# Head norms of q and k: sums of squares on TensorE transposes, or on 32x32 turns in VectorE and a DRAM round trip

## The chip, the cores and the metric

The kernel runs on one core of one Trainium2 chip. A core has five engines with queues of their own: PE (TensorE, matrix products; PEld is its weight load), DVE (VectorE), ACT (ScalarE), POOL (GpSimd) and SP (SyncE, which here issues nearly all DMAs). Each works through its own list of instructions in order and waits on semaphores for the others. The metric is the device time of one execution in microseconds. The median of three runs of the kernel before is 1879.47 us (1879.23 to 1879.48).

## The reference

One layer of a decoder trunk on 512 tokens with 2048 channels. What matters here is the QK normalisation in two of its three token mixers:

```python
def _rms_norm(x, g):
    xf = x.astype(jnp.float32)
    y = xf * lax.rsqrt(jnp.mean(xf * xf, axis=-1, keepdims=True) + EPS)
    return (y * g.astype(jnp.float32)).astype(x.dtype)

h = _rms_norm(x, norm1_g[l])
proj = h @ w_in[l]
aq, ak, av, bu, bg, cq, ck, cv = jnp.split(proj, splits, axis=-1)
aq = _rms_norm(aq.reshape(B, S, A_HEADS, HEAD_DIM), a_q_g[l])     # 8 heads x 64
ak = _rms_norm(ak.reshape(B, S, A_HEADS, HEAD_DIM), a_k_g[l])
out_a = _dilated_mixture(aq, ak, av)
out_b = _conformer_conv(bu, bg, ...)
cq = _rms_norm(cq.reshape(B, S, C_Q_HEADS, HEAD_DIM), c_q_g[l])   # 16 heads x 64
ck = _rms_norm(ck.reshape(B, S, C_KV_HEADS, HEAD_DIM), c_k_g[l])  # 2 heads x 64
out_c, _ = _band_attention(cq, ck, cv, C_WINDOW - 1, sinks=c_sinks[l])
x = x + jnp.concatenate([out_a, out_b, out_c], axis=-1) @ w_out[l]
h2 = _rms_norm(x, norm2_g[l])
x = x + (jax.nn.silu(h2 @ w_gate[l]) * (h2 @ w_up[l])) @ w_down[l]
```

So each token needs, for each head of q and k, one over the root of the sum of 64 squares.

## The kernel before, in words

Activations are held with channels on the 128 partitions and the 512 tokens along the free axis, in tiles of 128x512. Every product is done in three float32r matmuls (`mm3`, lines 315 to 317): high by high, high by low, low by high part. The program runs through the first normalisation, the 30 projections of the list `PROJ`, the output projection (32 units), gate and up in a Strassen-like form (line 1081), and down (lines 1339 to 1341).

Each projection makes one tile of 128 output channels, which for q and k is two heads of 64. The 17 tiles that need head norms are `ck`, `cq0` to `cq7`, `ak0` to `ak3` and `aq0` to `aq3`. A projection is two units of weights with 8 steps each; after every second step the kernel calls `ticks.tick()`, so a projection has 8 ticks. Everything that isn't a projection is hung on these ticks: `ticks.after(n, f)` puts `f` into the program n + 1 ticks later. A tick fixes only where an instruction stands in the order of its engine, not when it runs; an engine that is late stays late, and PE stops only where it reads something that isn't there yet.

`head_scales` does this for each of the 17 tiles: ACT copies the bank to `raw` (line 578); SQ = 3 ticks later PE turns `raw` in four 128x128 transposes into a bank (`flip`, line 583), so that tokens lie on partitions; a tick later ACT squares it (line 588); a tick later DVE sums groups of 64 (line 593) and adds 64 times epsilon (line 595); a tick later POOL takes the power of -1/2 (line 600). The result `r` is 128 tokens x 4 token blocks x 2 heads.

For q (`do_q`), `r` is used as the scale of the scores: DVE first reads it in `top` (line 741), ACT in `exps` (line 751). The q tile itself is split in high and low parts, and two DMAs (lines 628, 629, `twin`) put the low part below the high one. For k (`do_k`) two ticks after the power ACT spreads `r` over 64 columns (`widen`, line 640), a tick later PE turns it back (line 647), DVE multiplies `raw` by it (line 652), ACT and DVE split it (657, 662), and eight DMAs (line 670) lay out the copies. `attention` takes its first tick from `box["q at"]`, `box["k at"]` and the head before it; the scores are on lines 731 and 732.

SP's queue carries the weight loads (`pump`, line 254), these `twin` DMAs, and near the end of the stage the loads of x for the residual (line 913). A weight load waits for DVE to have finished with the buffer (line 264). DVE also runs the 124 taps of the depthwise convolution (lines 524, 526) over the whole stage, about one every two ticks.

Of the kernel before, what the change touches and what calls it, by code (L numbers as in the profile page):

```python
# [9 lines left out]
F32 = mybir.dt.float32  # L10
# [3 lines left out]
AF = mybir.ActivationFunctionType  # L14
ALU = mybir.AluOpType

P = 128
T = 512
NT = T // P
D = 2048  # L20
KT = D // P
HD = 64
# [13 lines left out]
TAP_PAUSE = (197, 211)  # L36


SQ, VD, TD, EV = 3, 4, 2, 1


C_TICKS = (1, 6, 2, 2, 2, 2, 5, 1, 3)
# [74 lines left out]
def kernel(ctx: ExitStack, tc: tile.TileContext, xT, wi, wo, wgu, wd, cst_in, outT):  # L117
    nc = tc.nc
    cp = ctx.enter_context(tc.tile_pool(name="consts", bufs=1))
# [16 lines left out]
    ticks = Ticks()  # L136

    def slot(name, dt=F32, cols=T):
        return sp.tile([P, cols], dt, name=name, tag="s")

    def bank(name, cols=T, pool="banks"):
        return psum[pool].tile([P, cols], F32, name=name, tag="b")
# [51 lines left out]
    for p in GU_ORDER:  # L194
        for m in range(2):
# [4 lines left out]
    bufs = {"A": dict(zip(("21", "11", "s", "22"), ("21a", "22a", "sa", "22b"))),  # L200
            "B": dict(zip(("21", "11", "s", "22"), ("21b", "11", "12", "sb")))}
# [6 lines left out]
    for t, (g, r) in enumerate(DOWN):  # L208
# [7 lines left out]
        for k in ("21A", "11A", "21B", "11B", "22A", "22B", "12A", "12B"):  # L216
            c = k[2]
# [20 lines left out]
        bufs = {c: {"21": b["s"], "s": b["21"], "11": b["22"], "22": b["11"]} for c, b in bufs.items()}  # L238

    splits = {}  # L240
    at = {"entry": 0, "split": 0, "use": 0}
# [95 lines left out]
    b = bank("idle")  # L337
    for i in range(WARM):
        nc.tensor.matmul(b, idle, idle[:, None, :].to_broadcast([P, NT, P]), start=True, stop=True)
    b = idle = None  # L340

    nhalf = cp.tile([P, 8], F32, name="nhalf")
# [3 lines left out]
    ident = cp.tile([P, P], F32, name="ident")  # L346
# [18 lines left out]
        return b  # L365

    def small(name, cols=NT):
        return cp.tile([P, cols], F32, name=name, tag="small", bufs=24)


    mult_a = slot("mult_a")
# [47 lines left out]
    def token_scale(acc, n, name, b=None):  # L419

        v, r = small(name + "v"), small(name + "r")
        if b is None:

            t, b = bank(name), v
            for i in range(NT):
                nc.tensor.transpose(t[:, i * P:(i + 1) * P], acc[:, i * P:(i + 1) * P], ident)
            nc.vector.tensor_reduce(v, t.rearrange("p (a b) -> p a b", b=P), axis=mybir.AxisListType.X, op=ALU.add)
        else:
            stat_rows(b[:, :, None], acc, ones)
        nc.vector.tensor_scalar(v, b, 1.0 / n, EPS, op0=ALU.mult, op1=ALU.add)  # L430
        nc.gpsimd.tensor_tensor(r, v, nhalf[:, :NT], op=ALU.pow)  # L431
        return v, r
# [46 lines left out]
    c64 = cp.tile([P, NT], F32, name="c64")  # L479
# [7 lines left out]
    def project(name):  # L487
        b = bank(name, pool="tiles")
        for half in range(2):
            wh, wl = next_unit()  # L490
            for kk in range(8):
                k = 8 * half + kk
                s = slice(kk * P, (kk + 1) * P)
                mm3(b, wh[:, s], wl[:, s], h_hi[k], h_lo[k], k == 0, k == KT - 1)
                if kk == 3:
                    lows_now()
                if kk % 2 == 1:
                    ticks.tick()
        return b
# [75 lines left out]
    def head_scales(b, name, then):  # L575

        raw = slot(name + "raw")
        nc.scalar.copy(raw, b)

        def flip():  # L580
            b2 = bank(name + "f")
            for i in range(NT):
                nc.tensor.transpose(b2[:, i * P:(i + 1) * P], raw[:, i * P:(i + 1) * P], ident)
            ticks.after(1, square, b2)

        def square(b2):
            sq = slot(name + "sq")
            nc.scalar.activation(sq, b2, AF.Square)
            ticks.after(1, total, sq)

        def total(sq):
            v = cp.tile([P, NT, 2], F32, name=name + "v", tag="hsv", bufs=3)
            nc.vector.tensor_reduce(v.rearrange("p a b -> p (a b)"), sq.rearrange("p (a b) -> p a b", b=HD),
                                    axis=mybir.AxisListType.X, op=ALU.add)
            nc.vector.tensor_add(v, v, c64[:, :, None].to_broadcast([P, NT, 2]))
            ticks.after(1, power, v)

        def power(v):
            r = cp.tile([P, NT, 2], F32, name=name + "r", tag="hsr", bufs=4)
            nc.gpsimd.tensor_tensor(r, v, nhalf.rearrange("p (a b) -> p a b", b=2), op=ALU.pow)  # L600
            then(r)

        ticks.after(SQ, flip)
        return raw

    def do_q(box, b, name):
        def then(r):
            box["rq"] = r

        raw = head_scales(b, name, then)  # L610
        box["q at"] = ticks.now + SQ + 6

        q = [slot(f"{name}{h}", F32R) for h in range(2)]
        lo = slot(f"{name}l", F32R)
        box["q"] = q
        one, two = HALF

        def high():
            nc.scalar.copy(q[0], raw)
            nc.scalar.copy(q[1][one], raw[two])  # L620
            ticks.after(1, low)

        def low():
            nc.vector.tensor_sub(lo, raw, q[0].bitcast(F32))
            ticks.after(1, twin)

        def twin():
            nc.sync.dma_start(q[0][two].bitcast(F32), lo[one].bitcast(F32))
            nc.sync.dma_start(q[1][two].bitcast(F32), lo[two].bitcast(F32))
        ticks.after(1, high)  # L630

    def do_k(box, b, name, gi):
        def then(r):
            ticks.after(2, widen, r)

        raw = head_scales(b, name, then)
        box["k at"] = ticks.now + SQ + TD + 12
        def widen(r):
            wide = slot(name + "wide")
            nc.scalar.copy(wide.rearrange("p (a b c) -> p a b c", a=NT, b=2),  # L640
                           r[:, :, :, None].to_broadcast([P, NT, 2, HD]))
            ticks.after(1, flip, wide)

        def flip(wide):
            b2 = bank(name + "t")
            for i in range(NT):
                nc.tensor.transpose(b2[:, i * P:(i + 1) * P], wide[:, i * P:(i + 1) * P], ident)
            ticks.after(1, scale, b2)

        def scale(b2):  # L650
            k = slot(f"{name}k")
            nc.vector.scalar_tensor_tensor(k, raw, gqk[:, gi:gi + 1], b2, op0=ALU.mult, op1=ALU.mult)
            ticks.after(1, high, k)

        def high(k):
            hi = slot(f"{name}hi", F32R)
            nc.scalar.copy(hi, k)
            ticks.after(1, low, k, hi)

        def low(k, hi):  # L660
            lo = slot(f"{name}lo", F32R)
            nc.vector.tensor_sub(lo, k, hi.bitcast(F32))
            ticks.after(1, twin, hi, lo)

        def twin(*parts):
            box["k"] = [[slot(f"{name}{'hl'[i]}{h}", F32R) for i in range(2)] for h in range(2)]
            for h in range(2):
                for to, part in zip(box["k"][h], parts):
                    for at in HALF:
                        nc.sync.dma_start(to[at].bitcast(F32), part[HALF[h]].bitcast(F32))  # L670
# [209 lines left out]
    for name in PROJ[HEAD4:]:  # L880
        kind, what, j = name[0], name[1], name[2:]
        if name == PROJ[-2]:
            for n, row in enumerate(ROWS[:8]):
                ticks.after(6 + n, split_mix, row)
        b = project(name)
        if kind == "b":
            ticks.after(0, glu_u if what == "u" else glu, int(j), b)
            continue
        if kind == "c":
            box = Heads(shared) if j else shared  # L890
        else:
            box = boxes.setdefault(j, {})
        if what == "k":
            do_k(box, b, name, 1 if kind == "c" else 0)
        elif what == "v":
            do_v(box, b, name)
        else:
            do_q(box, b, name)
        if what == "q":
            if kind == "a":  # L900
                boxes.pop(j)
            attention(kind, box, mix, kind + j, (int(j), int(j) + 8) if kind == "c" else None)
    b = box = boxes = shared = None
# [81 lines left out]
    for half in range(2):  # L985
        for i, n in enumerate(OUT_ORDER[half]):
            if half == 1 and i == 2:
                open_banks(banks=2, high=2)
            b = bank(f"o{half}_{n}", pool="tiles")
            wh, wl = next_unit()  # L990
            for kk in range(8):
                k = 8 * half + kk
# [22 lines left out]
    b = m_hi = m_lo = r1b = mult_a = bias_a = bias_c = None  # L1015
# [33 lines left out]
    flip = [1]  # L1049
# [177 lines left out]
    for g in range(2 * NP):  # L1227
        p, m = GU_ORDER[g // 2], g % 2
# [257 lines left out]
```

## Time and profile before

| | us |
|---|---|
| median of the runs | 1879.47 |
| span of the profiled execution | 1877.5 |
| PE busy | 1871.1 |
| PEld busy | 1603.6 |
| DVE busy | 1469.3 |
| ACT busy | 1345.5 |
| POOL busy | 1066.3 |

The profiled execution lasted 1877.5 us from its first to its last instruction; the runs' median is 2.0 us above that. Start times below are in us from the start of the span. A row of a timeline gives the start, the length, the engine, the line, the operation with what it writes and reads, the count of merged instructions, and in brackets how long the engine stood idle before it and for whom. The granted TensorE clock is full in every slice of the page.

### The profile page before, as it was taken

Reading aid. Unit: us, or ns where it says so; the run is one execution under the profiler, and the core shown is the slowest. Engines: PE = TensorE matmul, PEld = TensorE weight load, DVE = VectorE, ACT = ScalarE, POOL = GpSimd, SP = SyncE. Lnnn points to the kernel's source line nnn. Section 1 sums busy time; section 2 is a strip of 40 time slices with the busy share of each in tenths; the row PEclk is TensorE's granted clock in tenths of the full one; section 3 lists DMA queues with packets and bytes.
Section 4 is the critical chain, followed back from the end, with each engine's and each line's share of the span. In section 5 each row is a group of like instructions: output and inputs, shape, how many; then the busy total and the mean of one; then the engine's idle time right before and its main releaser. Section 6 shows DMA issues by size and latency. Waiting matters only on the chain.

```text
span 1877.5 us, 28378 instructions
## 1 busy us (share of the span) xinstructions
PE 1871.1 (100%) x9722; PEld 1603.6 (85%) x9722; DVE 1469.3 (78%) x2468; ACT 1345.5 (72%) x1872; POOL 1066.3 (57%) x666
## 2 busy tenths in 40 slices
PE   9999999999999999999999999999999999999999
PEld 7888888888888888888888888888888888888887
DVE  6789978999679777777777777778777778677777
ACT  6356645453457888888878888788888877778775
POOL 0111011010002888788878888787787788879775
PEclk9999999999999999999999999999999999999999
DMA  7232242333342445555555554555546967666545
GB/s 271 92 126 81 82 122 89 113 117 125 119 145 98 146 145 173 157 177 185 158 167 157 181 184 158 164 157 186 167 152 234 328 219 240 224 212 238 199 142 113
DMA packets 201089, 307.11 MB, mean 164 GB/s; under 512 B 62960, under 2 KB 112752, under 8 KB 200944
## 3 DMA queue, kind: packets, MB, share of 16 engines
q1 hardware_dynamic: 200800, 305.28, 50.4%
q8 instruction: 77, 1.26, 0.3%
q14 instruction: 68, 0.56, 0.1%
q10 hardware_dynamic: 144, 0.01, 0.0%
HBM read 243.89 MB, written 52.95 MB: 158 GB/s over the span
## 4 chain that ended last, share of the span: by engine, by line
PE 99%; DMA 0%; SPq 0%; ACT 0%; DVE 0%; issue 0%; DVEq 0%
PE out L1081 46%; PE out L1339 7%; PE out L1341 7%; PE out L1340 7%; PE o L315 3%; PE o L316 3%; PE o L317 3%; PE cq L315 2%; PE cq L317 2%; PE cq L316 2%; PE av L315 1%; PE ak L315 1%; PE av L317 1%; PE aq L317 1%; PE aq L315 1%; PE ak L317 1%
## 5 line engine op out<-in xcount | busy, mean ns | idle before, releaser
L1081 PE MATMUL out<-h,wh 128*128 128x512 f32 x2464 | 588.6, 391 | 0.0
L1081 PEld LDWEIGHTS out<-h,wh 128*128 128x128 f32 x2464 | 453.1, 188 | 87.1
L1081 PEld LDWEIGHTS out<-h,wl 128*128 128x128 f32 x2464 | 315.9, 191 | 12.0
L1081 PE MATMUL out<-h,wl 128*128 128x256 f32 x2464 | 319.7, 283 | 0.0
L1339 PE MATMUL out<-wh,a 128*128 128x512 f32 x620 | 240.6, 388 | 0.0
L1341 PE MATMUL out<-wh,a 128*128 128x512 f32 x620 | 240.6, 388 | 0.0
L1340 PE MATMUL out<-wl,a 128*128 128x512 f32 x620 | 240.6, 388 | 0.0
L286 ACT CAST wh<-w 128x1024 fp32r<-128x1024 f32 (+2 forms) x94 | 96.7, 1030 | 119.6 <-PE o L316 51.2
L264 DVE TENSOR_TENSOR wl<-w,wh 128x1024 fp32r<-128x1024 f32 (+2 forms) x95 | 112.8, 1187 | 37.2 <-ACT wh L286 37.0
L1341 PEld LDWEIGHTS out<-wh,a 128*128 128x128 f32 x620 | 116.4, 188 | 23.9
L1340 PEld LDWEIGHTS out<-wl,a 128*128 128x128 f32 x620 | 116.4, 188 | 23.8
L1339 PEld LDWEIGHTS out<-wh,a 128*128 128x128 f32 x620 | 116.4, 188 | 23.7
L1349 DVE TENSOR_TENSOR y<-y,out 128x512 f32<-128x512 f32 x164 | 106.3, 683 | 25.3 <-PE out L1341 23.5
L526 DVE SCALAR_TENSOR_TENSOR y<-bu,cst,y 128x511 f32<-128x511 f32 (+14 forms) x120 | 87.6, 730 | 0.4
L315 PE MATMUL cq<-hh,wh 128*128 128x512 f32 x128 | 51.1, 400 | 0.0
L315 PE MATMUL o<-mh_c,wh 128*128 128x512 f32 x128 | 51.1, 400 | 0.0
L317 PE MATMUL cq<-hh,wl 128*128 128x512 f32 x128 | 50.1, 391 | 0.0
L317 PE MATMUL o<-mh_c,wl 128*128 128x512 f32 x128 | 50.0, 391 | 0.0
L316 PE MATMUL cq<-hl,wh 128*128 128x512 f32 x128 | 50.0, 391 | 0.0
L316 PE MATMUL o<-ml_c,wh 128*128 128x512 f32 x128 | 50.0, 390 | 0.0
L431 POOL TENSOR_TENSOR lvr<-lvv,nhalf 128x4 f32<-128x4 f32 x1 | 1.9, 1920 | 74.5 <-DVE lvv L430 74.5
L182 POOL TENSOR_TENSOR w('s', 'g0')_5681<-w('21', 'g0')_5527,w('22', 'g0')_5525 128x1024 f32<-128x1024 f32 x1 | 2.5, 2456 | 69.0 <-DVE wl L264 69.0
(3016 smaller groups left out, 4945.2 us busy)
## 6 DMA issues: line engine op xcount, KB each, us to landing
od<-a SPq DMA_DIRECT2D x154, 256.0 KB, 4.8
a<-od SPq DMA_DIRECT2D x154, 256.0 KB, 5.5
w<-in_wi SPq DMA_DIRECT2D x58, 512.0 KB, 3.5
w<-in_wo SPq DMA_DIRECT2D x32, 512.0 KB, 3.5
x<-in_xT SPq DMA_DIRECT2D x16, 256.0 KB, 6.9
xr<-in_xT SPq DMA_DIRECT2D x16, 256.0 KB, 3.7
x2d<-xr SPq DMA_DIRECT2D x16, 256.0 KB, 2.0
z<-x2d SPq DMA_DIRECT2D x64, 64.0 KB, 3.7
```

Source lines behind the costliest of these rows:

```text
L182: nc.gpsimd.tensor_add(out[:, :n], raws[key[a]][0][:, :n], raws[key[b]][0][:, :n])
L264: fn(*args)
L286: (nc.vector.tensor_copy if u == 0 else nc.scalar.copy)(hi[:, :n], t[:, :n])
L315: nc.tensor.matmul(out, wh, xh, start=start, stop=False)
L316: nc.tensor.matmul(out, wh, xl, start=False, stop=False)
L317: nc.tensor.matmul(out, wl, xh, start=False, stop=stop)
L526: nc.vector.scalar_tensor_tensor(yconv[j][:, i:], hconv[j][:, :T - i], c, yconv[j][:, i:], op0=ALU.mult, op1=ALU.add)
L1081: nc.tensor.matmul(out, lhs[:, s], rhs, start=begin, stop=x is xs[-1] and low == flip[0], skip_group_check=True)
L1339: nc.tensor.matmul(b[:, lo:hi], x[:, high], wh[:, s], start=start, stop=False, skip_group_check=True)
L1340: nc.tensor.matmul(b[:, lo:hi], x[:, high], wl[:, s], start=False, stop=False, skip_group_check=True)
L1341: nc.tensor.matmul(b[:, lo:hi], x[:, low], wh[:, s], start=False, stop=last, skip_group_check=True)
L1349: getattr(eng, op)(t, t, src)
```

## The change

`head_scales` no longer transposes on PE. ACT squares `raw` itself, one tick after the copy. DVE then sums over channels while it turns 32x32 blocks (`apply_transpose=True`): each block of 32 channels and 32 tokens becomes 32 sums, with tokens on partitions. The result `part` has, on partition 32 a + i, the sum over channel quarter a of token 32 l + i of block b, in 16 columns. Four DMAs write these to a small DRAM tile, ordered so that one DMA reads them back with tokens on 128 partitions; POOL adds the two quarters of each head, adds epsilon, and takes the power. The constants of the ticks change with it: SD = 7 stands for the ticks up to the power, `q at` goes from 9 ticks to 10 and `k at` from 17 to 18. The pool of small tiles shrinks from 24 to 8 buffers.

```diff
-SQ, VD, TD, EV = 3, 4, 2, 1
+SD, VD, EV = 7, 4, 1
...
-        return cp.tile([P, cols], F32, name=name, tag="small", bufs=24)
+        return cp.tile([P, cols], F32, name=name, tag="small", bufs=8)
...
-        def flip():
-            b2 = bank(name + "f")
-            for i in range(NT):
-                nc.tensor.transpose(b2[:, i * P:(i + 1) * P], raw[:, i * P:(i + 1) * P], ident)
-            ticks.after(1, square, b2)
-
-        def square(b2):
+        def square():
             sq = slot(name + "sq")
-            nc.scalar.activation(sq, b2, AF.Square)
+            nc.scalar.activation(sq, raw, AF.Square)
             ticks.after(1, total, sq)
 
         def total(sq):
-            v = cp.tile([P, NT, 2], F32, name=name + "v", tag="hsv", bufs=3)
-            nc.vector.tensor_reduce(v.rearrange("p a b -> p (a b)"), sq.rearrange("p (a b) -> p a b", b=HD),
-                                    axis=mybir.AxisListType.X, op=ALU.add)
-            nc.vector.tensor_add(v, v, c64[:, :, None].to_broadcast([P, NT, 2]))
-            ticks.after(1, power, v)
-
-        def power(v):
+            part = cp.tile([P, NT, NT], F32, name=name + "p", tag="hsp", bufs=3)
+            nc.vector.tensor_reduce(part.rearrange("p l b -> p b l"),
+                                    sq.rearrange("p (b l c) -> p b l c", b=NT, l=NT),
+                                    axis=mybir.AxisListType.X, op=ALU.add, apply_transpose=True)
+            ticks.after(1, leave, part)
+
+        def leave(part):
+            d = tc.dram_tile([P, 2 * NT * 2], F32, name=name + "d")
+            for a in range(4):
+                nc.sync.dma_start(d.rearrange("(l i) (a b) -> i l a b", i=32, a=4)[:, :, a], part[32 * a:32 * a + 32])
+            ticks.after(2, back, d)
+
+        def back(d):
+            t = cp.tile([P, 2, 2, NT], F32, name=name + "t", tag="hst", bufs=3)
+            nc.sync.dma_start(t.rearrange("p h a b -> p (h a b)"), d)
+            ticks.after(2, power, t)
+
+        def power(t):
             r = cp.tile([P, NT, 2], F32, name=name + "r", tag="hsr", bufs=4)
-            nc.gpsimd.tensor_tensor(r, v, nhalf.rearrange("p (a b) -> p a b", b=2), op=ALU.pow)
+            by_head = r.rearrange("p b h -> p h b")
+            nc.gpsimd.tensor_add(by_head, t[:, :, 0], t[:, :, 1])
+            nc.gpsimd.tensor_add(r, r, c64[:, :, None].to_broadcast([P, NT, 2]))
+            nc.gpsimd.tensor_tensor(r, r, nhalf.rearrange("p (a b) -> p a b", b=2), op=ALU.pow)
             then(r)
 
-        ticks.after(SQ, flip)
+        ticks.after(1, square)
...
-        box["q at"] = ticks.now + SQ + 6
+        box["q at"] = ticks.now + SD + 3
...
-        box["k at"] = ticks.now + SQ + TD + 12
+        box["k at"] = ticks.now + SD + 11
```

## The prediction

> **What bounds the kernel now.** I read the page first, then the waits of PE, then busy time by stretches, and last the timeline of the stage that the change touches.
>
> ```profile
> span 1877.5 us, 28378 instructions
> PE 1871.1 (100%) x9722; PEld 1603.6 (85%) x9722; DVE 1469.3 (78%) x2468; ACT 1345.5 (72%) x1872; POOL 1066.3 (57%) x666
> PE 99%; DMA 0%; SPq 0%; ACT 0%; DVE 0%; issue 0%; DVEq 0%
> ```
>
> The chain that ended last is PE for 99% of the span: a microsecond of PE work taken out is a microsecond won, as long as PE then finds its inputs in time. The waits of PE over the whole span (those over 0.5 us after its warm-up):
>
> ```profile
> PE in L315 <- ACT wh L286: 0.7, 1, 0.7
> PE sides L1304 <- DVE y L1318: 0.7, 1, 0.7
> ```
>
> These lie in the first projections and at the very end. The stage of the head norms runs from about 60 to 420 us (columns: the stretch, its length, then busy time of PE, PEld, DVE, ACT and POOL, clock, DMA share, GB/s):
>
> ```profile
> 60.00:420.00 360.00, 360.00 (x1870) 305.14 (x1869) 314.58 (x788) 197.26 (x401) 38.58 (x21) 1.00 0.34 103
> ```
>
> PE has no gap in it, at full clock; DVE stands idle for 45 us of 360 and POOL for 321. So all the other engines deliver before PE asks, and the question is what margin they deliver with.
>
> **What it removes.** Seventeen groups of four transposes on PE. One, in PE's timeline:
>
> ```profile
> 77.77 0.39 PE L317 MATMUL cq<-hh,wl 128*128 128x512 f32 x1
> 78.00 0.60 PE L583 MATMUL ckf<-ident,ckraw 128*128 128x128 f32 x4
> 78.36 0.48 PE L315 MATMUL cq<-hh,wh 128*128 128x512 f32 x1
> 78.67 0.39 PE L316 MATMUL cq<-hl,wh 128*128 128x512 f32 x1
> 78.90 0.40 PE L317 MATMUL cq<-hh,wl 128*128 128x512 f32 x1
> ```
>
> Matmuls overlap, so starts count, not lengths. From 77.77 to 78.67 is 0.90 us, of which two 512-column matmuls at the pitch of 0.23 (78.67 to 78.90) take 0.46: the group costs 0.44. The chain's own row for the last group says the same:
>
> ```profile
> 412.87 0.44 PE aq3f L583 x4
> ```
>
> 17 x 0.44 = 7.5 us. If only the step to the next matmul counted (78.36 - 78.00 = 0.36) it would be 6.1; if the whole length of 0.60 counted, 10.2. I take 7.5, which two views give. Nothing is added on PE. The banks that `flip` held come free with it.
>
> **What it adds on the other engines.** The old end of the norm and the nearest row to the new sum:
>
> ```profile
> 92.69 0.68 DVE L593 TENSOR_REDUCE cq0v<-cq0sq 128x8 f32<-128x512 f32 x1
> 93.40 0.17 DVE L595 TENSOR_TENSOR cq0v<-cq0v,c 128x8 f32<-128x8 f32 x1
> 93.65 2.06 POOL L600 TENSOR_TENSOR cq0r<-cq0v,nhalf 128x8 f32<-128x8 f32 x1 [10.42 <-DVE cq0v L595]
> L1202 DVE STREAM_TRANSPOSE zt<-z x16: 702/704/705, 726.6 to 1311.1; 128x512 f32<-128x512 f32 x16
> ```
>
> A sum with a turn isn't in the trace. The plain sum of the same 128x512 took 0.68, a turn of 128x512 took 0.70; between 0.68 (both in one pass) and 1.38 (one after the other) I take 0.70, since the turn alone goes at the pace of one pass. DVE then changes by 17 x (0.70 - 0.68 - 0.17) = -2.5 us, or by +9.0 at the upper end, against 45 us idle: no cost either way. ACT's square reads the copy in place of the bank, the same 128x512, and only moves forward. POOL gets two small adds a tile. The page's adds of 128x1024 on POOL take 2.46:
>
> ```profile
> L182 POOL TENSOR_TENSOR w('s', 'g0')_5681<-w('21', 'g0')_5527,w('22', 'g0')_5525 128x1024 f32<-128x1024 f32 x1 | 2.5, 2456 | 69.0 <-DVE wl L264 69.0
> ```
>
> Eight columns must be far below that and below the power (2.06); I take 0.2 each, with 0 and 2.06 as ends. POOL is idle, so this is latency alone.
>
> **The round trip.** SP issues five more DMAs a tile, 85 in all. Rows for the price of an issue and for the time from issue to landing (the DMA view: count, size each, median us to landing):
>
> ```profile
> 88.18 0.53 SPq L628 DMA_DIRECT2D cq<-cq0l  x1
> 88.76 0.58 SPq L629 DMA_DIRECT2D cq<-cq0l  x1
> cq<-cq0l SPq DMA_DIRECT2D x2, 128.0 KB, 2.3
> w<-in_wi SPq DMA_DIRECT2D x58, 512.0 KB, 3.5
> z<-x2d SPq DMA_DIRECT2D x64, 64.0 KB, 3.7
> ckl<-cklo SPq DMA_DIRECT2D x4, 128.0 KB, 4.0
> a<-od SPq DMA_DIRECT2D x154, 256.0 KB, 5.5
> ```
>
> The four writes start 0.58 apart, so the last starts 1.7 after the first. Small DMAs with nothing before them land in 2.3; behind a weight load, which SP's order has just ahead of most reads back, they can hardly land before its 3.5. I take 2.3 for the write and 3.5 for the read, 5.8 a round trip. The bounds are 4.6 (2.3 twice) and 11.0 (the 5.5 of `a<-od` twice).
>
> The Trainium skill, DMA: Bandwidth & Descriptors, section Specifications, speaks against the write: pieces below 512 B are written by read-modify-write, and these are 16 B. No row of this trace shows what that costs. If it doubled the write's 2.3, the round trip would be 8.1 and the sum below would end near 1877 instead of 1872.
>
> From the end of the old sum (92.69 + 0.68 = 93.37) to the end of the power (95.71) were 2.3 us. Now: 1.7 + 5.8 + 2 x 0.2 + 2.06 = 10.0, so 7.7 more. Against that the sum moves three ticks forward (tick 5 to 2) and its users one tick back, four ticks in all. A tick, from copies eight ticks apart:
>
> ```profile
> 72.76 0.59 ACT L578 COPY ckraw<-ck 128x512 f32<-128x512 f32 x1 [3.48 <-PE ck L317]
> 84.11 0.59 ACT L578 COPY cq0raw<-cq 128x512 f32<-128x512 f32 x1 [4.59 <-PE cq L317]
> 223.24 0.59 ACT L578 COPY ak2raw<-ak 128x512 f32<-128x512 f32 x1 [0.65 <-PE ak L317]
> 237.21 0.59 ACT L578 COPY cq4raw<-cq 128x512 f32<-128x512 f32 x1 [2.28 <-PE cq L317]
> ```
>
> 11.35 / 8 = 1.42 us early, 13.97 / 8 = 1.75 with attention between. Four ticks give back 5.7 for `ck`, 7.0 for the four `ak`: the result comes 2.0 and 0.7 later against its use. The margins before, for the k tiles, where PE itself waits for the widened result:
>
> ```profile
> 81.15 2.07 POOL L600 TENSOR_TENSOR ckr<-ckv,nhalf 128x8 f32<-128x8 f32 x1 [18.28 <-DVE ckv L595]
> 85.54 0.62 ACT L640 COPY ckwide<-ckr 128x512 f32<-128x512 f32 x1
> 86.64 0.60 PE L647 MATMUL ckt<-ident,ckwide 128*128 128x128 f32 x4
> 234.85 1.64 POOL L600 TENSOR_TENSOR ak2r<-ak2v,nhalf 128x8 f32<-128x8 f32 x1 [22.71 <-DVE ak2v L595]
> 238.64 0.62 ACT L640 COPY ak2wide<-ak2r 128x512 f32<-128x512 f32 x1
> 239.68 0.49 PE L647 MATMUL ak2t<-ident,ak2wide 128*128 128x128 f32 x3
> ```
>
> `ck`: 85.54 - 83.22 = 2.3 ahead of ACT, and 86.64 - 86.16 = 0.5 ahead of PE, 2.8 together. `ak2`: 2.15 + 0.4 = 2.6. Taking out a transpose group between brings PE 0.44 nearer. What is left: 2.8 - 2.0 - 0.4 = 0.4 for `ck`, 2.6 - 0.7 - 0.4 = 1.5 for `ak2`, which I use for all four. No stall, but thin. For q the first reader is DVE; the tightest tile:
>
> ```profile
> 119.53 2.06 POOL L600 TENSOR_TENSOR cq3r<-cq3v,nhalf 128x8 f32<-128x8 f32 x1 [23.82 <-DVE cq3v L595]
> 124.31 0.16 DVE L741 SCALAR_TENSOR_TENSOR c3d<-c3d,cq3r 128x2 f32<-128x2 f32 x1
> ```
>
> 2.7 of margin against at most 2.0; a wait there would hold up the weights' low parts and the softmax behind it on DVE, and take first from its idle 45 us.
>
> **What queues behind the new waits on SP.** The read back waits on SP for its write to land, and what SP has next waits too. Weights are loaded several buffers ahead. Late can be the eight copies of `ck`, which come right after the read back of `cq0`:
>
> ```profile
> 87.47 0.68 DVE L624 TENSOR_TENSOR cq0l<-cq0raw,cq 128x512 fp32r<-128x512 f32 x1
> 90.08 1.10 SPq L670 DMA_DIRECT2D ckh<-ckhi  x2
> 91.27 1.21 SPq L670 DMA_DIRECT2D ckl<-cklo  x2
> 98.48 0.22 PE L731 MATMUL c0s<-ckh,cq 128*128 128x128 f32 x1
> ```
>
> The fourth copy started at 91.9 and landed 4.0 later at 95.9, 2.6 before the scores. After: the sum of `cq0` takes DVE's place of 87.47 and ends at 88.2, the last write starts at 89.9 and lands at 92.2, the first copy goes out at about 92.6 instead of 90.1, so the fourth lands at 98.4. The scores move to 98.48 + 1.42 - 2 x 0.44 = 99.0. That leaves 0.6; with a write of 3.7 it is a stall of 0.8. I charge 0.4.
>
> **The sum.** 1877.5 - 7.5 + 0.4 = 1870.4 for the span; the runs' median stood 2.0 above it, so 1872.4.
>
> **The rivals.** *A slow round trip that eats the gain.* Let the round trip be x longer than 5.8. The stalls are (x - 0.4) for `ck` and 4 (x - 1.5) for the `ak`, 5x - 6.4, and cancel the 7.5 at x = 2.8, a round trip of 8.6 or 4.3 a hop. For it: `ckl` at 4.0 a hop, which gives 8.0, x = 2.2, 4.6 us of stalls, 1876.6 (with the 0.4). Against it: those copies stand eight in a row of 128 KB, these are 2 to 8 KB. The Trainium skill's rule on small pieces (DMA: Bandwidth & Descriptors, Specifications) would act here.
>
> *Slower than before.* The same place, five `widen` steps on ACT and the transposes of line 647 behind them, with hops like `a<-od`: 11.0, x = 5.2, stalls of 19.6, 1892. It decides from 4.3 us a hop on; 0.2% slower needs 4.7. For it: nothing in the trace writes 16 B pieces. Against it: `a<-od` moves 256 KB.
>
> *The turn in DVE is dear.* 1.38 in place of 0.70 adds 11.6 us of DVE ahead of the low parts and softmax. If all of that reached PE: 1884; none: 1872. With 45 us idle I give half at most, 1878.
>
> *It doesn't do what it says.* PE loses the groups but waits elsewhere as long, since the whole of attention moves a tick against the projections: 1879.5. Against it: PE waits nowhere in the stage now, and one tick is all that its order moves.
>
> **How the numbers follow.** Forecast 0.60, between 1871 and 1874; the slow round trip 0.14, of which a third stays faster; slower 0.14; dear turn 0.05; no effect 0.07. About 0.2% (3.8 us) is what a measurement of this kernel can tell from no change. Faster (below 1875.7): 0.60 + 0.05 + 0.02 = 0.67; slower: 0.14 + 0.01 = 0.15; same: 0.18. The range: below, 1870.0 takes in most of the dearer transposes (10.2 would give 1869.7); above, 1879.5 takes in the slow round trip and no effect, and leaves out about 0.17.
>
> **What would show it.** No line 583 on PE, and PE in 60 to 413 us still 100% busy in the shorter stage. The sum with a turn near 0.70. Landings near 2.3 and 3.5; the power ending before `widen` starts. PE waits on line 647 or 731 would show a rival; a wait of SP on the write of more than 4.3 would make the prediction wrong.

## The result and the profile after

| | before | after |
|---|---|---|
| median of 5 runs each, us | 1879.38 (1879.23 to 1879.48) | 1872.85 (1872.28 to 1873.11) |
| span of the profiled execution, us | 1877.5 | 1870.5 |
| PE busy, us | 1871.1 | 1864.2 |
| DVE busy, us | 1469.3 | 1466.2 |
| POOL busy, us | 1066.3 | 1072.9 |

The ratio is 0.9965, with a 95% interval of 0.9953 to 0.9977: 6.5 us less. Of the page after, the span, the engines and the chain that ended last:

```profile
span 1870.5 us, 28387 instructions
PE 1864.2 (100%) x9654; PEld 1597.0 (85%) x9654; DVE 1466.2 (78%) x2451; ACT 1345.4 (72%) x1872; POOL 1072.9 (57%) x700
PE 100%; DVE 0%; issue 0%; ACT 0%; DVEq 0%
```

PE has 68 instructions fewer (17 x 4) and is busy 6.9 us less; the span is 7.0 shorter. So nothing of what came off PE was given back as a wait. The view by stretches of the changed kernel shows the stage itself (columns as in the prediction):

```profile
60.00:412.50 352.50, 352.50 (x1801) 298.32 (x1800) 311.81 (x772) 197.01 (x401) 42.95 (x52) 1.00 0.36 106
```

PE is busy in all of it, at full clock, as before, and the list of PE's waits has no row between 60 and 420 us. Where the time came out is read from the chain in order of time, at the first long piece behind the stage (start, length). Before:

```profile
607.18 846.16 PE out L1081 x4864
1874.10 0.27 ACT end L1307
```

and after:

```profile
599.49 846.16 PE out L1089 x4864
1866.41 0.27 ACT end L1315
```

The piece is equally long and starts 7.69 us earlier, and the last step of ACT comes 7.69 earlier as well. The span has 7.0 of that only: the two DMAs that carry the last output took longer to issue this time, 1.17 in place of 0.89, and the span ended 3.8 us after ACT's last step in place of 3.1. In SP's timeline, before:

```profile
1874.32 0.89 SPq L1326 DMA_DIRECT2D out_T<-end  x2
```

after:

```profile
1866.71 1.17 SPq L1334 DMA_DIRECT2D out_T<-end  x2
```

Those are not touched by the change. Behind the long piece the seven runs below have 424.2 to 424.8 us, the kernel before 424.2 and the changed kernel 424.9, so this 0.7 us is what one execution may differ by from another.

The new path of the first k tile, in the timeline of the changed kernel:

```profile
76.03 0.71 DVE L587 TRANSPOSE_TENSOR_REDUCE ckp<-cksq 128x16 f32<-128x512 f32 x1
76.76 2.55 SPq L595 DMA_DIRECT2D ckd<-ckp  x4
80.57 0.34 SPq L600 DMA_DIRECT2D ckt<-ckd  x1
83.59 0.20 POOL L606 TENSOR_TENSOR ckr<-ckt 128x8 f32<-128x8 f32 x1 [20.79 <-DMA ckt<-ckd]
84.16 1.64 POOL L608 TENSOR_TENSOR ckr<-ckr,nhalf 128x8 f32<-128x8 f32 x1
85.83 0.62 ACT L648 COPY ckwide<-ckr 128x512 f32<-128x512 f32 x1 [0.76 <-POOL ckr L608]
87.43 0.60 PE L655 MATMUL ckt<-ident,ckwide 128*128 128x128 f32 x4
```

Read it from the end: the widened result ends at 86.45, PE takes it at 87.43, so 1.0 us is left. ACT did wait 0.76 us for the power, and that wait stopped there. ACT waited for it at four of the five k tiles (0.3 to 2.1 us), so the prediction's sign that the power ends before ACT's widening starts held there only because ACT waited; PE's margin took that up. The times from issue to landing, first of all the writes (line 595), then of all the reads back (line 600):

```profile
DMA to landing us min/median/max: 1.4/1.5/3.2
```

```profile
DMA to landing us min/median/max: 3.0/3.1/4.4
```

### The profile page after: what moved, and what is told of

Same layout as the page of the kernel before. It is cut to its first block, busy times and chain, and to the rows that moved or that the text cites. A ratio compares the mean times of both kernels' runs of the same rounds, so it can differ in the third digit from the quotient of the medians.

```text
span 1870.5 us, 28387 instructions
## 1 busy us (share of the span) xinstructions
PE 1864.2 (100%) x9654; PEld 1597.0 (85%) x9654; DVE 1466.2 (78%) x2451; ACT 1345.4 (72%) x1872; POOL 1072.9 (57%) x700
## 4 chain that ended last, share of the span: by engine, by line
PE 100%; DVE 0%; issue 0%; ACT 0%; DVEq 0%
PE out L1089 46%; PE out L1349 7%; PE out L1348 7%; PE out L1347 7%; PE o L315 3%; PE o L317 3%; PE o L316 3%; PE cq L315 2%; PE cq L317 2%; PE cq L316 2%; PE aq L317 1%; PE aq L315 1%; PE ak L315 1%; PE av L315 1%; PE ak L317 1%; PE av L316 1%
```

## The experiments

Each is an edit of the changed kernel. The theory to be tried: all of the gain is PE's time in the 17 groups, 0.44 us each; the round trip is long but covered by its ticks. The rivals: that the trip holds something up and costs part of the gain, or that the gain comes from another move of the change (the order of attention, freed banks).

### The transposes put back, unread

```diff
+        def flip():
+            b2 = bank(name + "f")
+            for i in range(NT):
+                nc.tensor.transpose(b2[:, i * P:(i + 1) * P], raw[:, i * P:(i + 1) * P], ident)
+
+        ticks.after(3, flip)
         ticks.after(1, square)
```

> The changed kernel with the 17 groups of four transposes put back on PE, three ticks after the copy, into a bank that nobody reads. Theory (the whole gain is PE time, 0.44 us a group, the rest of the change costs nothing): 7.5 us above the changed kernel, 1880.4, within 0.2% of the kernel before. Rival (the gain comes from moving the sum and the waits to other places): it stays near 1873.

Measured: 1880.16 us (1879.68 to 1880.63), ratio to before 1.0005 (0.9996 to 1.0013), span 1878.4. The page and the chain of this run:

```profile
PE 1872.2 (100%) x9722; PEld 1603.5 (85%) x9722; DVE 1465.3 (78%) x2451; ACT 1345.4 (72%) x1872; POOL 1071.6 (57%) x700
607.43 846.16 PE out L1095 x4864
```

PE has the 9722 instructions of before again, and the long piece starts 7.9 us later than in the changed kernel. Everything else of the change is still in it, and the time is that of before. So the gain is the time of PE's groups; DVE's sum with a turn, the trip and the moved ticks bring nothing. That they cost nothing is shown only as closely as the interval allows: the median stands 0.9 us above that of before (1879.26 in that round).

### The round trip left out

```diff
-            ticks.after(1, leave, part)
+            ticks.after(5, power, part.rearrange("p (h a) b -> p h a b", h=2))
```

> The changed kernel without the DRAM round trip: POOL adds and takes the power of the sums as they lie after the turn, at the same tick as before, so the tokens' scales are the wrong ones and the five DMAs a tile are left out. Theory (the round trip is wholly hidden): the time of the changed kernel, 1872.9, within 0.1%. Rival (SP's waits or the late results cost part of the gain, the 0.4 us that I charged or more): 1 to 3 us faster, 1870 to 1872.

Measured: 1871.95 us (1871.72 to 1872.17), ratio 0.9960 (0.9947 to 0.9972), span 1870.4 against 1870.5 with the trip. The result lies within the 0.1% of the theory and in the rival's 1870 to 1872 as well, so the time alone does not decide. The intervals overlap, and the long piece of the chain even starts later than with the trip:

```profile
599.94 846.17 PE out L1089 x4864
```

That is 0.45 us against 599.49, with no wait of PE in the stage in either, and nearly all of it arose ahead of the stage: the first tile's copy (line 578) started at 73.05 here and at 72.67 in the changed kernel. The 85 DMAs cost at most some 0.9 us by the medians, and nothing that the profile can place. Whether that 0.9 is a cost or the spread between occasions stays open.

### A second round trip at the same ticks

```diff
             nc.sync.dma_start(t.rearrange("p h a b -> p (h a b)"), d)
-            ticks.after(2, power, t)
+            d2 = tc.dram_tile([P, 2 * NT * 2], F32, name=name + "e")
+            t2 = cp.tile([P, 2, 2, NT], F32, name=name + "u", tag="hsu", bufs=3)
+            nc.sync.dma_start(d2, t.rearrange("p h a b -> p (h a b)"))
+            nc.sync.dma_start(t2.rearrange("p h a b -> p (h a b)"), d2)
+            ticks.after(2, power, t2)
```

> The changed kernel with a second round trip behind the first, one write and one read of the same 8 KB, at the same ticks. From the changed kernel's trace the write lands in about 1.5 us and the read in 3.1, so the result is about 5 us later; PE's margin on the turned k scale there is 1.0, 1.5, 0.9, 0.9 and 1.3 us for ck, ak2, ak0, ak1 and ak3. Theory (what is late stops ACT at the widening and PE at the five turns behind it): 25 - 5.5 = 19 us of waits of PE on line 655's group, a time of 1888 to 1896. Rival (later work has so much slack that the five places don't add up): under 1880. Second rival (SP's blocked queue does the harm, by late weights or late copies): PE waits at projections or scores.

Measured: 1897.93 us (1896.2 to 1899.99), ratio 1.0099 (1.0085 to 1.0113), span 1894.4, 23.9 above the changed kernel, and more than the 1888 to 1896 expected. The waits of PE in the stage (engine, tile, line, released by: us in total, times, longest):

```profile
PE ak3t L659 <- ACT ak3wide L652: 4.6, 1, 4.6
PE ak2t L659 <- ACT ak2wide L652: 3.8, 1, 3.8
PE ak0t L659 <- ACT ak0wide L652: 3.2, 1, 3.2
PE ckt L659 <- ACT ckwide L652: 2.2, 1, 2.2
PE ak1t L659 <- ACT ak1wide L652: 1.5, 1, 1.5
PE c0s L744 <- DMA ckl<-cklo: 0.9, 1, 0.9
```

The five k tiles stall PE, in the place that the prediction named for a slow trip; of the second rival there are only 1.1 us, at the first scores. The second trip was shorter than the 5 us expected, and still the time is longer. For the first tile the wait is what the margin says: the second trip took 3.2 us (POOL's first add at 86.80 in place of 83.59); less the 1.0 that was left, that is 2.2. For three of the later tiles it is longer than 3.2 less their margin: at `ak2` the writes started 9.0 us of PE's own time ahead of its turn (234.09 to 246.96, less the wait of 3.83) where the changed kernel has 11.25 (225.96 to 237.21). The writes wait for DVE's sum, and that came 8.1 us later than in the changed kernel (233.35 against 225.22) where PE's own turn came 5.9 later. DVE has waits here that the changed kernel lacks, among them 2.9 us at `c3` for late scales (line 753); that these made the sum late was not tried.

With 0.4 at two smaller ones, the waits sum up to 16.6; 7.3 us of the 23.9 are still missing. Most of them stand in the matmuls behind the waits. PE's timeline after the wait of `ck`:

```profile
90.20 0.48 PE L315 MATMUL bu<-hh,wh 128*128 128x512 f32 x1
90.52 0.39 PE L316 MATMUL bu<-hl,wh 128*128 128x512 f32 x1
...
90.98 0.60 PE L315 MATMUL bu<-hh,wh 128*128 128x512 f32 x1
91.38 0.63 PE L316 MATMUL bu<-hl,wh 128*128 128x512 f32 x1
91.81 0.63 PE L317 MATMUL bu<-hh,wl 128*128 128x512 f32 x1
...
93.94 0.61 PE L316 MATMUL bu<-hl,wh 128*128 128x512 f32 x1
94.37 0.42 PE L317 MATMUL bu<-hh,wl 128*128 128x512 f32 x1
94.62 0.39 PE L315 MATMUL bu<-hh,wh 128*128 128x512 f32 x1
```

From 90.98 to 94.37 the starts are 0.43 apart in place of 0.23. The granted clock by stretches says why (eighth number; before it the busy times):

```profile
91.00:94.40 3.40, 3.40 (x10) 2.62 (x9) 3.17 (x6) 1.99 (x3) 0.00 (x0) 0.50 0.20 29
94.40:97.00 2.60, 2.60 (x13) 2.14 (x12) 1.84 (x3) 0.00 (x0) 0.00 (x0) 1.00 0.84 251
249.00:252.00 3.00, 3.00 (x16) 2.77 (x16) 2.63 (x4) 1.66 (x3) 0.00 (x0) 0.60 0.35 61
252.00:255.00 3.00, 3.00 (x16) 2.49 (x15) 3.00 (x6) 1.56 (x3) 0.00 (x0) 1.00 0.69 207
```

The clock falls to a half and comes back some 3.5 us later. It reads 0.50 in 249.00 to 251.40, 279.00 to 282.10 and 412.20 to 415.20 too, behind the three longer waits, and 1.00 in 334.20 to 338.00, behind the one of 1.5 us. PE's timeline has starts 0.43 apart after the waits of 2.2, 3.2, 3.8 and 4.6 us, and none after those of 1.5 and 0.9. The stretch shown costs 1.6 us (nine steps in 3.64, at 0.23 each 2.07); four like it would make 6.4 of the missing 7.3, an estimate from this one.

### Two ticks taken back

```diff
-SD, VD, EV = 7, 4, 1
+SD, VD, EV = 5, 4, 1
...
-            ticks.after(2, back, d)
+            ticks.after(1, back, d)
...
-            ticks.after(2, power, t)
+            ticks.after(1, power, t)
```

> The changed kernel with one tick in place of two between the writes and the read back and between the read and the power, and the uses of the result two ticks earlier (SD = 5). Two ticks are 2.8 us early and 3.5 us with attention between. Theory (the schedule's two extra ticks are what hides the trip): PE waits 1.9 to 2.6 us at each of the five turns, about 11 us in all, less about 1 us each where the read no longer stands behind a weight load on SP: 1878 to 1884. Rival (the ticks are spare): 1872 to 1874.

Measured: 1874.41 us (1873.85 to 1874.87), ratio 0.9974 (0.9963 to 0.9985), span 1872.5: far less than the 1878 to 1884 of the theory, and just above the rival's 1872 to 1874. (Inside a function that a tick calls, as here, `ticks.after(n, f)` puts `f` n ticks later; the n + 1 given above holds for calls between ticks.) All waits of PE in the stage, and the landing of the reads back:

```profile
PE c0s L740 <- DMA ckl<-cklo: 1.0, 1, 1.0
PE ckt L655 <- ACT ckwide L648: 0.8, 1, 0.8
```

```profile
DMA to landing us min/median/max: 1.5/1.8/3.3
```

The first k tile is late, once at its transposes and once at the scores that its copies feed; the four `ak` aren't. One tick earlier the read back goes out ahead of the weight load that stood before it on SP, and lands in 1.8 in place of 3.1, so part of what the two ticks took away came back as a shorter trip. From the first write's start to POOL's first add, `ak0` took 4.63 us in place of 7.95, `ak1` 4.83 in place of 7.27, `ak2` 4.76 in place of 6.91; `ck` took 6.01 in place of 6.83, with its four writes slower to go out (3.15 against 2.55), and `ak3` 5.65 in place of 6.25. The waits of 0.8 and 1.0 explain 1.8 of the span's 2.0, and the clock stayed at 1.00 in both places.

### The two ticks for the first k tile alone

```diff
-            ticks.after(2, back, d)
+            ticks.after(2 if name == "ck" else 1, back, d)
...
-            ticks.after(2, power, t)
+            ticks.after(2 if name == "ck" else 1, power, t)
...
-        box["q at"] = ticks.now + SD + 3
+        box["q at"] = ticks.now + SD + 1
...
-        box["k at"] = ticks.now + SD + 11
+        box["k at"] = ticks.now + SD + (11 if name == "ck" else 9)
```

> The first k tile keeps the changed kernel's ticks; the other 16 tiles read their sums back one tick earlier and take the power another tick earlier, and their k and q are due two ticks earlier. Theory (the spare ticks are needed by the first k tile alone; with both ticks taken from all tiles TensorE waited 0.8 us at its turn and 1.0 us at the first scores, and nowhere else): no wait of TensorE in the stage, 1872.9 us as in the changed kernel. Rival (some other tile needs them, and its wait was hidden behind the first k tile's): a wait of 0.5 us or more at one of the four later k tiles, 1873.5 us or more.

Measured: 1872.64 us (1872.24 to 1872.99), ratio 0.9964 (0.9951 to 0.9976): the changed kernel's time, and no wait at any k tile. So the four `ak` had no wait that was hidden behind `ck`'s. But the theory's "no wait in the stage" failed: PE did wait once, where neither expected it. In this run's timeline:

```profile
116.14 0.59 SPq L637 DMA_DIRECT2D cq<-cq3l  x1
117.98 0.30 PE L739 MATMUL c3s<-ckh,cq 128*128 128x128 f32 x1 [0.76 <-DMA cq<-cq3l]
```

in the changed kernel:

```profile
116.11 0.59 SPq L637 DMA_DIRECT2D cq<-cq3l  x1
120.47 0.31 PE L739 MATMUL c3s<-ckh,cq 128*128 128x128 f32 x1
```

The copies of q leave at the same time in both, behind the four writes on SP, but PE comes to the scores at 117.22, 3.3 us sooner than the 120.47, and after the wait starts them 2.5 sooner: with q's due date two ticks earlier it is these copies, not the scales, that come last. So the ticks are needed by the first k tile for its scales, and by this q tile for its copies.

### The other transposes of k sent through DRAM too

The k tiles have a second group of transposes: the scales, widened by ACT, are turned so that channels are on partitions. Here DVE turns the 128x32 block that holds them, four DMAs write it as rows, and two read each head's row back on 64 partitions; `widen` and the transposes behind it are gone. POOL also clears the block before it takes the power into it.

```diff
...
+        def turn(r):
+            rt = cp.tile([P, 32], F32, name=name + "rt", tag="hsw", bufs=1)
+            nc.vector.transpose(rt, r)
+            d = tc.dram_tile([2, NT, P], F32, name=name + "w")
+            for a in range(4):
+                nc.sync.dma_start(d.rearrange("h b (a c) -> (h b) a c", a=4)[:, a], rt[32 * a:32 * a + 2 * NT])
+            ticks.after(2, fetch, d)
+
+        def fetch(d):
+            wide = slot(name + "wide")
+            flat = d.rearrange("h b c -> h (b c)")
+            for h in range(2):
+                nc.sync.dma_start(wide[HALF[h]], flat[h:h + 1].to_broadcast([HD, T]))
+            ticks.after(2, scale, wide)
...
```

Once for the four `ak`:

> For the four a heads' k tiles the scales go a second time through DRAM, as rows that are read back on 64 partitions each, and the four TensorE transposes that spread them are gone too (16 matmuls fewer). k is due two ticks later. Theory (each group off TensorE is worth 0.44 us, and a trip that has its ticks costs nothing): 4 x 0.44 = 1.8 us less than the changed kernel, 1871.1 us, no wait of TensorE in the stage. Rival (two ticks are too few for a read of 256 KB behind a weight load, so that VectorE stands at the product with k and the scores come late): a wait of TensorE of 1 us or more at the a heads' scores and 1873 us or more.

and once for all five:

> As the run with the four a heads' k tiles, with the first k tile (of the c heads) sent the same way, its k due two ticks later. Theory: 5 x 0.44 = 2.2 us less than the changed kernel, 1870.7 us, no wait of TensorE. Rival (the first k tile has no ticks to spare: in the run with two ticks fewer TensorE waited for it at its turn and at its scores): a wait of 1 us or more at the first scores of the c heads, and a time above that of the run that leaves this tile as it is.

Measured: 1869.84 us (1869.14 to 1869.97), ratio 0.9948 (0.9936 to 0.9961), and 1869.38 us (1868.81 to 1870.01), ratio 0.9947 (0.9933 to 0.9960). PE waits nowhere in the stage in either. The chain's long piece starts, with four groups gone and with five:

```profile
597.51 846.16 PE out L1114 x4864
```

```profile
596.93 846.16 PE out L1114 x4864
```

1.98 and 2.56 us ahead of the changed kernel, 0.5 a group, against 1.8 and 2.2 expected. The medians are 3.0 and 3.5 below it, which is more than came off PE in the stage. The surplus of about a microsecond is not a gain that the profile places in the stage: 0.6 of it is that the changed kernel's profiled execution was its fastest (1872.28 against a median of 1872.85), and the two spans differ by 0.4 and 0.5 more behind the long piece. Neither rival came about: PE has no wait at the scores, and leaving out the first tile's group as well was not slower. At `ak2`, with the four gone:

```profile
236.94 1.34 SPq L659 DMA_DIRECT2D ak2w<-ak2rt  x4
240.52 1.12 SPq L666 DMA_DIRECT2D ak2wide<-ak2w  x2
243.96 0.75 DVE L685 SCALAR_TENSOR_TENSOR ak2k<-ak2raw,gqk,ak2wide 128x512 f32<-128x512 f32 x1 [2.41 <-DMA ak2wide<-ak2w]
```

DVE does wait 2.4 us for the read, and PE waits nowhere all the same; whether k's due date two ticks later was needed for that was not tried. Both versions beat the changed kernel, whose fastest run was 1872.28, by more than the runs of either differ.

## Why the prediction was right

*PE's groups.* 7.5 us from starts in the timeline; the chain shows 7.69, and putting the groups back undoes it. The step between starts of neighbours was the right measure: the group's own 0.60 would have given 10.2.

*The sum with a turn.* 0.70 from a plain turn; 0.71 measured. That rules out the rival of a dear turn: DVE is busy 3.1 us less, where 2.5 was worked out.

*The round trip.* Mis-sized, on the safe side: 2.3 for the write was 1.5, 3.5 for the read was 3.1, so 4.6 in place of 5.8, the lower bound. The guess that the read stands behind the weight load was right, and the run with two ticks taken back shows the price of that place, 3.1 against 1.8. The prediction asked what it would be if the rule of the Trainium skill (DMA: Bandwidth & Descriptors, section Specifications) on pieces below 512 B doubled the write's 2.3; the 16 B pieces landed in 1.5, so no such price shows here.

The small terms held: the four writes start about 0.43 apart in the median (0.58 taken; `ck`'s four took 2.55 in all), and POOL's adds take mostly 0.20 each.

*The margins at PE.* 0.4 was worked out for `ck`, and 1.0 is left; for `ak2` 1.5, and 1.5 is left (237.21 less the end of the widened result at 235.72). Using `ak2` for all four was too kind to another. Here is `ak0` in the changed kernel:

```profile
262.62 0.62 ACT L648 COPY ak0wide<-ak0r 128x512 f32<-128x512 f32 x1 [2.08 <-POOL ak0r L608]
264.09 0.60 PE L655 MATMUL ak0t<-ident,ak0wide 128*128 128x128 f32 x4
```

264.09 - 263.24 = 0.85 us.

*The charged stall of 0.4 us.* It didn't happen: PE had no wait at the scores of c0. The first copy went out at 92.33 (92.6 worked out), but these copies landed in 2.8 us (the median of the DMA view) where the 4.0 of before had been taken over. The scores started at 98.78 (99.0). That the place is tight was right: with two ticks fewer PE waited 1.0 us there.

*The sum.* The forecast was right by its mechanism, PE's groups. That the span came out at 1870.5 against 1870.4, so close, was luck, errors that cancel: 0.4 for a stall that wasn't there and 0.2 too little for the groups, against 0.7 at the last output's DMAs.

*The rivals.* None came about, but the second trip shows that the price of a slow one was wrong. Its 1876.6 for hops of 4.0 leaves out the 0.4 that it says is in it; with it, it is 1877.0. The larger fault is that the prediction let a wait cost its length. The trip was lengthened by 3.2 us, and against its own terms that is x = 3.2 - 1.2 (the trip was 1.2 shorter than taken) = 2.0, for which 5x - 6.4 gives 3.6 us of stalls. Measured were 16.6 of waits and 7.3 more, most of it in slow matmuls after them. A round trip 3.2 us longer cost far more than the gain: that run is 18.7 us slower than the kernel before.

## What to carry to other kernels

Where PE is the whole chain, matmuls removed are worth the distance between the starts of their neighbours, and anything that is off PE may be long as long as it has its ticks: five more DMAs a tile and a trip of 4.6 us cost PE no wait, and at most some 0.9 us in all. Before such a trade, list the margin of every place where PE takes the result, the smallest first; it was 0.85 to 1.5 us here, and each wait of 2.2 us or more cost some 1.6 us on top at the halved clock. When a small DMA shares its queue with bulk loads, look at its place in the order as well as at its tick: here one place earlier took 1.3 us off a landing of 3.1.

## What was not expected of the hardware

A wait of PE can cost more than its length. After waits of 2.2 to 4.6 us, matmuls of 512 columns started 0.43 apart for 3 to 3.5 us, at a granted clock of 0.50 where a stretch holds nothing else; after waits of 0.8 to 1.5 us they didn't. The Trainium skill, TensorE: Matmul & The Clock Gate, section HAM oscillation — how this bites in real kernels, warns of gaps of PE above some 3.4 us; the halved rate agrees, but here a gap of 2.2 us was enough.

A sum of 128x512 that also turns 32x32 blocks cost DVE 0.71, about as much as the plain sum (0.68) or the plain turn (0.70) alone.

Writes of 128 pieces of 16 B to DRAM landed in 1.5 us; a read back of 128 rows of 64 B took 1.8 ahead of the weight load and 3.1 right behind one of 512 KB on the same queue.
